# Seven-product MLP blocks: T1 and B22 weight quarters in large tiles instead of raw buffers

## The chip, the cores and the metric

The kernel runs on one core of a Trainium2 chip. The metric is device time in microseconds. Before the change three runs gave 951.79, 952.26 and 953.13 us; their median is 952.26 us. One more execution, recorded by the hardware profiler, took 955.36 us.

## The reference

One layer of a decoder trunk, batch 1, 512 tokens, width 1024, in float32. With h = RMSNorm(x):

- z = h @ W_in, cut into queries, keys, values and gates of a retention mixer (4 heads) and of a dilated windowed attention (3 groups of 4 heads);
- x = x + W_o(sigmoid(g_A) * (A @ W_A) + sigmoid(g_B) * (B @ W_B)), where A and B are the two mixers' results;
- x = x + W_down(relu(RMSNorm(x) @ W_up)^2), with W_up 1024 x 4096 and W_down 4096 x 1024;
- x = x + sigmoid(RMSNorm(x) @ W_pg) * (p @ W_pp), with p 512 x 256.

The change lies in the third line, the MLP.

## The kernel before, in words

**Precision.** Every float32 matrix product is made of three float32r products. A factor v is split into hi (v rounded to float32r, by ScalarE) and lo (v - hi, by VectorE); `mm3` (L259) issues hi·hi, hi·lo and lo·hi into the same accumulator (L262 to L264). In the profile `whi` and `wlo` are the parts of a weight unit (split at L250 and L251), `f` is a left factor's tile (split at L1300 and L1301), `pg` and `pa` are accumulators in PSUM, `x` is the residual stream, updated at L1286.

**Seven products.** Large products are done by a Strassen-like scheme (Winograd's form): both factors are cut into 2 x 2 quarters, and seven products of quarters or of their sums replace eight. On the weight's side the seven factors are B11, B21, B22, T1, T2, T3 and T4. They use storage in chains. T1 starts as the quarter B12, to which B11 is added; after T1's split B22 is accumulated into the same storage, which is T2; after T2's split B21 is accumulated, which is T4. B22 likewise becomes T3, when B12 is accumulated into it after its split. A factor of 512 x 512 is loaded and split in two units, u = 0 and u = 1, of 128 partitions x 1024 values (0.5 MB).

**Order.** In the MLP the products run in the order HALVES (L37): 1, 1, 5, 5, 2, 3, 3, 6, 6, 2, then 7 and 4 with both units at once. In units this is B11, B11, T1, T1, B21, B22, B22, T2, T2, B21, T3, T3, T4, T4, that is 14 units a block. The MLP has four rounds f, each with an up block (`up_products`, left factors h2, seven `f` tiles that all four rounds use) and a down block (`seven_gemm`, left factors U, seven `f` tiles made from the up block's results by relu and square). An up block turns the roles round: the weights are the stationary operand and the matmuls have 256 columns; in a down block the matmuls have 512 columns.

**Loading.** `plan_seven` (L171) writes the list of units. `fetch` (L199) allocates a unit's storage and issues its load on SyncE's queue (SP, L212). `ahead` (L217) keeps the splits two units ahead of use (three in some stretches, `AHEAD`), adds B11 into T1 on VectorE (L226, the `vector` argument holds "T1" in the MLP) and has GpSimd (POOL) issue the accumulating loads of a chain (L228). Such a load must wait for the split of what stood there before.

**Storage.** Raw units lie in the pool `wraw`: six buffers of 128 x 1024 values. Every one of the eight units of a block that are really loaded (B11, T1, B21, B22, two each) takes one; T1's stay taken until T4's split, B22's until T3's split. The splits' results lie in four buffers each (`wsp`). The pool `bigp` has 16 "big" tiles of 128 x 2048 values, from which the left factors h2 and U, the residual x (two tiles), zq, h3 and pp are taken.

**Who orders what.** The program is written against a planner. It places each instruction in the queue of its engine by priority in program order and by its own cost model, gives a tile a free slot of its pool, and adds the waits for a slot's former users. In some stretches (the update by w_o and the embedding's product, the last down block and all behind it) ScalarE and VectorE keep the written order (`manual_schedule`). SP holds only transfers and POOL in the MLP almost only the accumulating loads; both take theirs in order.

Of the kernel before, what the change touches and what calls it, by code (L numbers as in the profile page):

```python
# [11 lines left out]
F32 = mybir.dt.float32  # L12
# [5 lines left out]
P = 128  # L18
# [18 lines left out]
HALVES = ((1, 0), (1, 1), (5, 0), (5, 1)) + SEVEN[4:]  # L37
# [42 lines left out]
class Block:  # L80


    def __init__(self, ctx, tc, a):
        self.tc, self.nc, self.a = tc, tc.nc, a
        pool = lambda n, b, **k: ctx.enter_context(tc.tile_pool(name=n, bufs=b, **k))
        self.const = pool("const", 1)
        self.wraw = pool("wraw", 6)
        self.wsp = pool("wsp", 4)
        self.bigp = pool("bigp", 16)
        self.tmpp = pool("tmpp", 12)  # L90
        self.tabp = pool("tabp", 4)
        self.sm = pool("sm", 8)
        self.psg = pool("psg", 4, space=bass.MemoryType.PSUM)
        self.psa = pool("psa", 4, space=bass.MemoryType.PSUM)
        self.dram = pool("dram", 1, space=bass.MemoryType.DRAM)
        self.n = 0
        self.ev = 0
        self.clock = 0
        self.queue = []
        self.done = set()  # L100
        self.pinned = False
        self.hook = None
        self.chained, self.added = {}, {}
        self.spare = False
        self.plan, self.raws, self.loaded, self.used = [], [], [], 0

# [61 lines left out]
        for u in range(nk // 2):  # L168
            self.plan.append((w[r0 + 256 * u : r0 + 256 * (u + 1), c0 : c0 + 512], None if g0 is None else g0 + 2 * u))

    def plan_seven(self, w, r0, c1, c2, order, vector=()):  # L171

        cols = (c1, c2)
        q = lambda i, j, u: w[r0 + 512 * i + 256 * u : r0 + 512 * i + 256 * (u + 1), cols[j] : cols[j] + 512]
        n = len(self.plan)
        units = [(FACTOR[m], v) for m, u in order for v in ((0, 1) if u is None else (u,))]
        at = lambda name, u: n + units.index((name, u))
        for name, u in units:
            if name == "T1":
                src = q(0, 1, u) if name in vector else (q(0, 1, u), q(0, 0, u))  # L180
                if name in vector:
                    self.added[at("B11", u)] = at("T1", u), at("B11", u)
            elif name == "T4" and name in vector:
                self.added[max(at("B21", u), at("T2", u))] = at("T2", u), at("B21", u)
                src = (None, at("T2", u))
            elif name[0] == "B":
                src = q(int(name[1]) - 1, int(name[2]) - 1, u)
            else:
                prev, ij = {"T2": ("T1", (1, 1)), "T3": ("B22", (0, 1)), "T4": ("T2", (1, 0))}[name]
                k = at(prev, u)  # L190
                self.chained[k] = q(*ij, u)
                src = (None, k)
            self.plan.append((src, None))

    def plan_cols(self, w, c0, nk, g0=None):
# [3 lines left out]
    def fetch(self, n):  # L199
        while len(self.raws) < min(len(self.plan), n):  # L200
            src, g0 = self.plan[len(self.raws)]
            add = None
            if isinstance(src, tuple):
                src, add = src[0], src[1:]
            if src is None:
                self.raws.append((self.raws[add[0]][0], None))
                continue
            raw = self.wraw.tile([P, 1024], F32, tag="raw", name=self.nm("raw"))
            k = src.shape[0] // P
            raw = raw.rearrange("p (k n) -> p k n", k=k)  # L210
            rows = lambda v: v.rearrange("(k p) n -> p k n", p=P)
            self.nc.sync.dma_start(raw, rows(src))  # L212
            if add is not None:
                self.nc.gpsimd.dma_start(raw, rows(add[0]), accum_op=ALU.add)
            self.raws.append((raw, g0))
# [1241 lines left out]
    def make_plan(self):  # L1457
        a, w = self.a, self.w_in
        pairs = {1: (AV, AV + 512), 2: (RK, AV + 1024)}
        for g in range(NG):  # L1460
            for c in (AQ, AK):
                self.plan_rows(w, c + 512 * g, KD)
            if g:
                self.plan_seven(w, 0, *pairs[g], SEVEN, ("T1",))
        for c in range(2):
            self.plan_cols(w, RQ + 256 * c, KD)
        for c in (0, 512):
            self.plan_seven(w, 0, RV + c, RG + c, SEVEN, ("T1", "T4"))
        self.plan_mix()
        self.plan_seven(a["w_o"][0], 0, 512, 0, SEVEN)  # L1470
        for half in range(2):
            self.plan_rows(a["w_ple_proj"][0], 512 * half, 2)
        for f in range(NF // 2):
            self.plan_seven(a["w_up"][0], 0, 1024 * f + 512, 1024 * f, HALVES, ("T1",))
            self.plan_seven(a["w_down"][0], 1024 * f, 512, 0, HALVES, ("T1",))
        for half in range(2):
            self.plan_rows(a["w_ple_gate"][0], 512 * half, KD, g0=32)

# [38 lines left out]
```

## Time and profile before

| what | value |
|---|---|
| median of three runs | 952.26 us (951.79 to 953.13) |
| profiled execution, own time | 955.36 us |
| its span (first to last instruction) | 953.6 us |
| granted TensorE clock | 0.997 |
| TensorE busy | 943.3 us, 99% |
| VectorE busy | 718.4 us, 75% |
| ScalarE busy | 562.1 us, 59% |
| GpSimd busy | 159.5 us, 17% |
| DMA | 162.87 MB, mean 171 GB/s |

How to read it: times are microseconds; PE is TensorE's matmuls, PEld its weight loads, DVE VectorE, ACT ScalarE, POOL GpSimd and SP SyncE. A group of instructions is named by its line in the kernel, its engine and its tiles as out<-in. "A <- B" among the waits means that A's engine sat idle until B was done. The MLP's eight blocks lie between about 587 and 896 us of the span; the last product and the output follow.

### The profile page before, as it was taken

How to read it: one execution, taken by the hardware profiler on the slowest of the kernel's cores; microseconds unless marked ns; L12 is line 12 of the kernel's file. 1: busy time of each engine (PE TensorE's matmuls, PEld its weight loads, DVE VectorE, ACT ScalarE, POOL GpSimd, SP SyncE). 2: the span in 40 equal slices, each digit the busy share in tenths (PEclk: the TensorE clock that was granted, in tenths of full speed). 3: DMA queues.
4: the chain of work that ended last, by engine and by line, in shares of the span. 5: the costliest groups of instructions: out<-in, count | busy, mean ns of one | idle time of the engine just before them, and what ended most of it. 6: DMA issues, size and time to landing. Idle time of an engine off the chain costs nothing.

```text
span 953.6 us, 14325 instructions
## 1 busy us (share of the span) xinstructions
PE 943.3 (99%) x5357; PEld 826.2 (87%) x5357; DVE 718.4 (75%) x997; ACT 562.1 (59%) x1065; POOL 159.5 (17%) x140
## 2 busy tenths in 40 slices
PE   9999999999899999999999999999999999999998
PEld 6888888888788888999988888988998998998887
DVE  7789964766697849386937889799499689769953
ACT  5657775445745566576714446884494486467651
POOL 0322210222001112223012211111212302112100
PEclk9999999999999999999999999999999999999999
DMA  9953466258437645869737677868958968876911
GB/s 333 282 170 82 106 141 215 64 118 195 148 111 155 173 100 138 163 181 217 232 115 236 148 178 214 206 153 222 199 156 202 191 183 157 224 172 159 288 50 56
DMA packets 92549, 162.87 MB, mean 171 GB/s; under 512 B 8608, under 2 KB 20544, under 8 KB 92480
## 3 DMA queue, kind: packets, MB, share of 16 engines
q1 hardware_dynamic: 65168, 113.37, 36.4%
q0 software_dynamic: 23936, 46.14, 29.0%
q10 hardware_dynamic: 3376, 2.44, 0.9%
q8 instruction: 42, 0.69, 0.3%
q14 instruction: 27, 0.22, 0.1%
HBM read 153.49 MB, written 6.34 MB: 168 GB/s over the span
## 4 chain that ended last, share of the span: by engine, by line
PE 92%; DVE 3%; ACT 1%; issue 1%; DMA 1%; POOL 1%; SPq 0%; ACTq 0%; POOLq 0%; DVEq 0%
PE pg L264 25%; PE pg L262 25%; PE pg L263 25%; PE pa L264 3%; PE pa L263 3%; PE pa L262 3%; PE po L835 1%; PE ph L590 1%; DVE wlo L251 1%; PE pe L694 1%; PE sc L787 1%; PE ry L1083 1%; PE kv L1070 1%; PE ry L1085 1%; DVE ro L578 0%
## 5 line engine op out<-in xcount | busy, mean ns | idle before, releaser
L251 DVE TENSOR_TENSOR wlo<-raw,whi 128x1024 fp32r<-128x1024 f32 (+1 forms) x258 | 306.8, 1198 | 112.7 <-ACT whi L250 111.8
L250 ACT ACTIVATE whi<-raw 128x1024 fp32r<-128x1024 f32 (+1 forms) x257 | 266.3, 1041 | 212.1 <-PE pg L264 87.2
L263 PE MATMUL pg<-f,whi 128*128 128x256 f32 x384 | 108.7, 283 | 0.0
L264 PE MATMUL pg<-f,wlo 128*128 128x256 f32 x384 | 108.7, 283 | 0.0
L262 PE MATMUL pg<-f,whi 128*128 128x256 f32 x384 | 108.7, 283 | 0.0
L262 PE MATMUL pg<-whi,hh 128*128 128x512 f32 x248 | 98.6, 398 | 0.0
L264 PE MATMUL pg<-whi,hl 128*128 128x512 f32 x248 | 97.1, 392 | 0.0
L263 PE MATMUL pg<-wlo,hh 128*128 128x512 f32 x248 | 96.8, 390 | 0.0
L262 PE MATMUL pg<-whi,f 128*128 128x512 f32 x192 | 75.4, 393 | 0.0
L263 PE MATMUL pg<-wlo,f 128*128 128x512 f32 x192 | 74.8, 389 | 0.0
L264 PE MATMUL pg<-whi,f 128*128 128x512 f32 x192 | 74.8, 389 | 0.0
L262 PEld LDWEIGHTS pg<-f,whi 128*128 128x128 f32 x384 | 73.7, 192 | 0.2
L263 PEld LDWEIGHTS pg<-f,whi 128*128 128x128 f32 x384 | 73.7, 192 | 0.2
L264 PEld LDWEIGHTS pg<-f,wlo 128*128 128x128 f32 x384 | 73.7, 192 | 0.0
L228 POOL DMA_DIRECT2D raw<-in_w_in x32 | 38.9, 1216 | 197.8 <-DVE wlo L251 193.0
L264 PEld LDWEIGHTS pg<-whi,hl 128*128 128x128 f32 x248 | 46.6, 188 | 9.8
L263 PEld LDWEIGHTS pg<-wlo,hh 128*128 128x128 f32 x248 | 46.6, 188 | 9.2
L262 PEld LDWEIGHTS pg<-whi,hh 128*128 128x128 f32 x248 | 46.6, 188 | 9.2
L228 POOL DMA_DIRECT2D raw<-in_w_down x24 | 29.0, 1215 | 139.3 <-DVE wlo L251 108.2
L262 PE MATMUL pg<-whi,us 128*128 128x512 f32 x128 | 52.1, 407 | 0.0
L228 POOL DMA_DIRECT2D raw<-in_w_up x24 | 29.0, 1211 | 135.0 <-DVE wlo L251 124.7
L264 PE MATMUL pg<-whi,us 128*128 128x512 f32 x128 | 50.0, 391 | 0.0
(280 smaller groups left out, 2298.0 us busy)
## 6 DMA issues: line engine op xcount, KB each, us to landing
raw<-in_w_in SPq DMA_DIRECT2D x72, 512.0 KB, 4.1
raw<-in_w_in POOLq DMA_DIRECT2D x32, 512.0 KB, 6.2
raw<-in_w_up SPq DMA_DIRECT2D x32, 512.0 KB, 4.6
raw<-in_w_down SPq DMA_DIRECT2D x32, 512.0 KB, 4.6
raw<-in_w_up POOLq DMA_DIRECT2D x24, 512.0 KB, 6.6
raw<-in_w_down POOLq DMA_DIRECT2D x24, 512.0 KB, 5.9
x<-in_x SPq DMA_DIRECT2D x8, 512.0 KB, 8.2
raw<-in_w_ret_out SPq DMA_DIRECT2D x8, 512.0 KB, 3.8
```

Source lines behind the costliest of these rows:

```text
L228: self.nc.gpsimd.dma_start(raw, self.chained[i].rearrange("(k p) n -> p k n", p=P), accum_op=ALU.add)
L250: self.pin(nc.scalar.activation(R(hi[:, i]), raw[:, i], AF.Copy))
L251: nc.vector.tensor_tensor(R(lo[:, i]), raw[:, i], hi[:, i], op=ALU.subtract)
L262: t.matmul(ps, sh, mh, start=first, stop=False, skip_group_check=more)
L263: t.matmul(ps, sh, ml, start=False, stop=False, skip_group_check=more)
L264: t.matmul(ps, sl, mh, start=False, stop=last, skip_group_check=more)
L590: self.nc.tensor.transpose(ps[:, t * P : (t + 1) * P], rots[t][:, h * HD : (h + 1) * HD], self.ident)
L694: self.nc.tensor.transpose(ps[:, k * P : (k + 1) * P], e[:, k * P : (k + 1) * P], self.ident)
L787: nc.tensor.matmul(sc[:, h * P : (h + 1) * P], qT[:, h, rs], kT[:, h, rs], start=True, stop=True)
L835: nc.tensor.matmul(po[:, h * P : (h + 1) * P], v[:, vt, h * HD : (h + 1) * HD], pt, start=b == 0, stop=b == len(blocks) - 1)
L1070: nc.tensor.matmul(ps, kd[:, n, hs], v[:, n, c], start=True, stop=True)
L1083: nc.tensor.matmul(y, sT[0][:, r], v[:, i, c], start=True, stop=i == 0)
```

## The change

`plan_seven` gets one more argument, `wide`, a list of factor names. A unit of such a factor is noted in `self.wide` with the plan position of the factor's first unit. `fetch` then doesn't allocate a `wraw` buffer for it: the factor's first unit allocates one big tile (128 x 4 x 512 values), and each of its two units takes one half of it, rearranged to 128 x 1024 values. The MLP's plans pass ("T1", "B22"). T2, T3 and T4 stand in the storage of T1 and B22, as before, so they go along. The pools keep their sizes (six raw buffers, 16 big tiles); loads, additions and accumulating loads are the same ones in the same program order.

```diff
@@ plan_seven
-    def plan_seven(self, w, r0, c1, c2, order, vector=()):
+    def plan_seven(self, w, r0, c1, c2, order, vector=(), wide=()):
...
                 self.chained[k] = q(*ij, u)
                 src = (None, k)
+            if name in wide:
+                self.wide[len(self.plan)] = at(name, 0), u
             self.plan.append((src, None))
@@ fetch
-            raw = self.wraw.tile([P, 1024], F32, tag="raw", name=self.nm("raw"))
+            if len(self.raws) in self.wide:
+                n, u = self.wide[len(self.raws)]
+                if n not in self.pairs:
+                    self.pairs[n] = self.big("raw")
+                raw = self.pairs[n][:, 2 * u : 2 * u + 2].rearrange("p a b -> p (a b)")
+            else:
+                raw = self.wraw.tile([P, 1024], F32, tag="raw", name=self.nm("raw"))
@@ make_plan
-            self.plan_seven(a["w_up"][0], 0, 1024 * f + 512, 1024 * f, HALVES, ("T1",))
-            self.plan_seven(a["w_down"][0], 1024 * f, 512, 0, HALVES, ("T1",))
+            self.plan_seven(a["w_up"][0], 0, 1024 * f + 512, 1024 * f, HALVES, ("T1",), ("T1", "B22"))
+            self.plan_seven(a["w_down"][0], 1024 * f, 512, 0, HALVES, ("T1",), ("T1", "B22"))
```

More of the change, by code (lines that the diff above doesn't have):

```diff
@@ L103, in __init__ @@
         self.chained, self.added = {}, {}
+        self.wide, self.pairs = {}, {}
         self.spare = False
```

## The prediction

> **What bounds the kernel now.** I read the engine totals and the chain of waits on the page first. "pg" and "pa" are the accumulators of the matrix products.
>
> ```profile
> PE 943.3 (99%) x5357; PEld 826.2 (87%) x5357; DVE 718.4 (75%) x997; ACT 562.1 (59%) x1065; POOL 159.5 (17%) x140
> ...
> PE 92%; DVE 3%; ACT 1%; issue 1%; DMA 1%; POOL 1%; SPq 0%; ACTq 0%; POOLq 0%; DVEq 0%
> ```
>
> TensorE is busy for 943.3 of 953.6 us and makes 92% of the chain that ends last. The change only touches the MLP, so next I read the busy time in single blocks: the first up block, the first down block, and the next up and down (their borders are where the matmuls change from 256 to 512 columns).
>
> ```profile
> 586.87:627.18 40.31, 40.31 (x337) 40.31 (x336) 33.53 (x44) 35.25 (x58) 7.26 (x6) 1.00 0.83 205
> 627.18:665.29 38.11, 38.11 (x171) 31.54 (x169) 37.17 (x48) 21.61 (x28) 7.28 (x6) 1.00 0.85 194
> 665.29:705.60 40.31, 40.31 (x337) 40.31 (x336) 26.39 (x28) 26.43 (x37) 7.25 (x6) 1.00 0.77 183
> 705.60:743.97 38.37, 38.37 (x171) 31.38 (x169) 37.10 (x47) 21.80 (x29) 7.25 (x6) 1.00 0.82 191
> ```
>
> The columns are: length, busy PE, PEld, DVE, ACT and POOL, the granted clock (1.00), the share and GB/s of the DMA engines. PE is busy to the last hundredth. A busy PE could hide slow matmuls, so I also read the starts of matmuls in a down block and in an up block:
>
> ```profile
> 799.95 0.39 PE L262 MATMUL pg<-whi,f 128*128 128x512 f32 x1
> ...
> 804.94 0.39 PE L263 MATMUL pg<-wlo,f 128*128 128x512 f32 x1
> ```
>
> ```profile
> 589.74 0.28 PE L262 MATMUL pg<-f,whi 128*128 128x256 f32 x1
> ...
> 592.98 0.28 PE L262 MATMUL pg<-f,whi 128*128 128x256 f32 x1
> ```
>
> From 799.95 to 804.94 there are 22 starts after the first, 0.227 us apart; from 589.74 to 592.98 there are 27, 0.120 us apart. A down block has 14 weight units of 12 matmuls: 168 x 0.227 = 38.1 us. An up block has 14 of 24: 336 x 0.120 = 40.3 us. Both are the measured lengths, so these blocks hold nearly no hidden idle time. The exception is the second down block, 38.37 against 38.11: 0.26 us lost. What TensorE waits for from 560 us on is little (two answers of the waits view, for PE and for its weight loads):
>
> ```profile
> PE pg L262 <- ACT pp L533: 0.2, 1, 0.2
> ```
>
> ```profile
> PEld pg L262 <- ACT pp L533: 0.6, 1, 0.6
> PEld pg L263 <- DVE wlo L256: 0.5, 1, 0.5
> PEld pg L262 <- issue: 0.3, 1, 0.3
> PEld pg L262 <- ACT whi L250: 0.3, 1, 0.3
> PEld pg L262 <- DVE x L1286: 0.3, 1, 0.3
> ```
>
> None of these names a weight load. Against them stands what SyncE's queue waits for between 582 and 862 us:
>
> ```profile
> SPq L212 <- DVE wlo L251: 238.0, 53, 13.9
> ```
>
> The weight loads do wait for a free raw buffer: 53 times, 238 us. But no engine on the chain pays for it. The buffers are scarce, and scarce off the path.
>
> **The change, part by part.** *What is moved.* In each of the eight MLP blocks, T1 (B12 loaded, B11 added by DVE at L226, B22 and then B21 accumulated into it by POOL) and B22 (with B12 accumulated later) leave the raw pool. Each becomes one half-pair of a "big" tile. B11 and B21 stay in the six raw buffers. The instructions stay:
>
> ```profile
> raw<-in_w_up SPq DMA_DIRECT2D x32, 512.0 KB, 4.6
> raw<-in_w_down SPq DMA_DIRECT2D x32, 512.0 KB, 4.6
> raw<-in_w_up POOLq DMA_DIRECT2D x24, 512.0 KB, 6.6
> raw<-in_w_down POOLq DMA_DIRECT2D x24, 512.0 KB, 5.9
> ```
>
> There are 64 loads on SP, 48 accumulations on POOL and 16 additions of about 1.22 us on DVE before and after, of the same shapes. Removed and added work: 0 us. Compute operands remain contiguous rows of 1024 values, so I take no change in durations.
>
> *What is freed.* A block asks for four raw buffers instead of eight. B11 and B21 can therefore be loaded up to a block and a half ahead, and the 238 us of SP waits shrink or become waits for big tiles. Worth on the path: only PE idle time counts. Upper bound of a gain: 0.26 us (second down block) + 0.2 + 0.6 + 0.5 + 0.3 x 3 = 2.5 us if all of it vanished and none were counted twice. But the pp rows and the last stage's wlo L256 do not involve these buffers, and the 0.3 of x L1286 is probably part of the 0.26. What the change could reach is 0.26 + 0.3 (issue) + 0.3 (whi), about 0.9 us. I take 0.2.
>
> *What is added: demand on the big tiles.* There are 16. During the MLP seven hold the left factors of up, two the residual x; the seven left factors of down take the rest, exactly 16. T1 and B22 make 18, so something must wait. Big tiles seem to be handed out in program order: pp is written back by 596 us at the latest (589.6, its last store, and at most 8.0 to landing), but is loaded again into big tiles only at 895 us, just behind the first writes of h3, which stands before it in the program.
>
> ```profile
> L534 SPq DMA_DIRECT2D pp_dram<-pp x8: 319/320/350, 579.5 to 589.6; - x8
> L1439 SPq DMA_DIRECT2D pp<-pp_dram x2: 421/439/457, 895.0 to 895.5; - x2
> ...
> DMA to landing us min/median/max: 2.0/3.4/8.0
> ```
>
> So the splits of the last left factors wait for TensorE to finish products 1 and 5, and the next T1 for the end of product 3's first use (seven units into the block). That is 5.4, 10.9 and 19.1 us after the block's start (2, 4 and 7 units of 12 x 0.227 = 2.72 us). Today the last of those splits run at 715.59, 10 us in, and are used by products 7 and 4, 27 and 33 us in; the wait moves them by about a microsecond. Behind them on ScalarE stand the splits of the coming weight units:
>
> ```profile
> 715.59 1.66 ACT L1300 ACTIVATE f<-r 128x512 fp32r<-128x512 f32 x3
> ...
> 730.31 1.07 ACT L250 ACTIVATE whi<-raw 128x1024 fp32r<-128x1024 f32 x1 [1.65 <-PE pg L264]
> ```
>
> The unit split at 730.31 is T4's first half, product 4's first operand:
>
> ```profile
> 735.17 1.06 ACT L250 ACTIVATE whi<-raw 128x1024 fp32r<-128x1024 f32 x1 [3.79 <-DVE wlo L251]
> ...
> 736.26 1.23 DVE L251 TENSOR_TENSOR wlo<-raw,whi 128x1024 fp32r<-128x1024 f32 x1 [1.20 <-ACT whi L250]
> ...
> 737.41 0.74 DVE L1286 SCALAR_TENSOR_TENSOR x<-pg,f,x 128x512 f32<-128x512 f32 x1
> ...
> 738.30 0.47 PE L262 MATMUL pg<-whi,f 128*128 128x512 f32 x1
> ```
>
> TensorE first needs it at 738.30: 8.0 us after 730.31, less 1.07 and 1.23 of splitting, leaves 5.7 us of cover. Cost taken: 0; without that cover, the wait itself.
>
> *The tightest place.* The same rows show it. T4's second half is split at 735.17, 3.79 us after ScalarE fell idle. The row names wlo, but the accumulation that fills this unit landed just then. It is the second of the pair that POOL issues at 723.40; the next answer is that line's landings from 720 to 740:
>
> ```profile
> 723.40 2.49 POOL L228 DMA_DIRECT2D raw<-in_w_down  x2 [0.90 <-DVE wlo L251]
> ```
>
> ```profile
> DMA to landing us min/median/max: 5.6/6.3/10.4
> ```
>
> The second starts 1.2 us or so behind the first, near 724.7; with the longest landing, 10.4, that is 735.1. DVE takes its instructions in order, so the update x stands behind that wlo, and product 4 adds into the bank that x must have read. PE starts at 738.30 with 0.47 instead of 0.39. So the landing of T4's accumulation reaches TensorE with no slack in this block. DVE is busy 37.17 of 38.11 us in the first down block, so 0.94 us is a fair estimate of the slack elsewhere. What is late here is paid.
>
> Why 10.4 instead of 5.6? SP issues seven loads from 715.96 to 740.81, in a burst once B22's raw buffers come free:
>
> ```profile
> 715.96 24.85 SPq L212 DMA_DIRECT2D raw<-in_w_up  x7
> ```
>
> After the change the raw loads of this burst go earlier, and T1's pair goes when product 3's big tile is free: 705.6 + 19.1 = 724.7, the very moment of T4's accumulations; B22's pair follows with product 6's tile at 9 units, 730.1. One load fewer to one load more beside the accumulation: 0.52 MB at 194 GB/s is 2.7 us either way. Bounds: minus 0.26 us in all to plus 2.7 x 3 = 8.1 us for three blocks (in the fourth no further MLP weights are loaded). I take +0.2, near the lower end, because the same bytes pass per block and the burst loses B11's loads while it gains T1's.
>
> The Trainium skill, "DMA: Bandwidth & Descriptors", section "Queues, rings and completion order", says that each DMA engine takes turns between the queues it has work for, packet by packet. By it an accumulation next to loads gets about half of the engines, so, as an estimate, 5.6 us becomes about 10; the row of 10.4 agrees, and by that rule T1's pair at 724.7 speaks against the change.
>
> *The ends.* The first T1 pair, loaded now from 564.08, could wait for a big tile. Even issued when w_o's matmuls end and its left factors' tiles come free (574.62, the first matmul of the next product), the pair would land by 574.6 + 2 x 4.6 = 583.8, against the first addition at 581.57; that addition's unit is the third of the block, used at 586.87 + 2 x 2.88 = 592.6. Cost 0.
>
> ```profile
> 564.08 9.58 SPq L212 DMA_DIRECT2D raw<-in_w_up  x4
> ```
>
> ```profile
> 574.62 0.39 PE L262 MATMUL pg<-whi,ph 128*128 128x512 f32 x1
> ```
>
> ```profile
> 581.57 1.22 DVE L226 TENSOR_TENSOR raw<-raw,raw 128x1024 f32<-128x1024 f32 x1
> ```
>
> *Sum.* The profiled execution took 955.36 us, 1.76 more than its span and 3.1 more than the median of 952.26. 955.36 + 0 (instructions) - 0.2 (stalls) + 0.2 (accumulations) = 955.4; as a median, 952.3 us.
>
> **The rivals.** *Late accumulations (slower).* At product 4 of the first three down blocks one more load lies beside T4's accumulation: 2.7 us later, less 0.94 of slack, 1.76 x 3 = 5.3 us: 957.6. It decides from the point where T4's second landing is more than 0.94 us later in its block than now. For: DVE at 37 of 38 us, 10.4 against 5.6. Against: equal bytes.
>
> *Big tiles run out (slower).* If a T1 takes the tile that the last left factor needs, that split waits until 19.1 instead of about 11 us; 8.2 less 5.7 of cover is 2.5 a block: 959.8. Against: program order puts T1 behind it.
>
> *The stalls go (slightly faster).* 952.26 - 0.9 = 951.4, still no difference that can be told.
>
> *It does not do what it says.* If T1's place in the order holds SP's later loads back, nothing is earlier: 952.3.
>
> *Hidden headroom (faster).* If the array idled wherever no weights are loaded, a down block would hold 38.11 - 31.54 = 6.6 us, four of them 26: 926. The even starts, 0.227 us apart, speak against it. The Trainium skill, "Perfetto Trace Analysis", section "Identifying the Most-Contended Engine", holds weight-load time for the better measure than matmul time; by that rule there is room, by the starts there is none.
>
> **How the numbers follow.** A difference under 0.2% (1.9 us) can't be told from none here. Chances: forecast 0.58 and "does not do it" 0.06 (952.3), stalls go 0.10 (951.4), late accumulations 0.19 (957.6), tiles run out 0.04 (959.8), headroom 0.03 (926). Faster: 0.03 and 0.04 of the tails of the first three: 0.07. Slower: 0.23 less 0.03 of milder cases, 0.20. Same: 0.73. The range goes from 951.0, below the case of 951.4, to 957.0, which takes in most of the late accumulations; its bound of 8.1 us (960.4) and the headroom stay outside.
>
> **What would show it.** Right: blocks of 40.3 and 38.1 us; no PE wait that names a raw or a left factor; SP's 238 us much smaller. Wrong on accumulations: down blocks over 39 us with x L1286 ahead of the first matmul of product 4, and T4's landing over 11 us. Wrong on tiles: ScalarE's f L1300 waiting for PE. What I could not see is the order that the planner gives ScalarE and VectorE once tiles are released at other times; a bad order there makes the prediction wrong.

## The result, and the profile after

The changed kernel takes 958.71 us (median of four runs, 957.54 to 959.62) against 952.23 us for the kernel before: a ratio of 1.0066 with a 95% interval from 1.0049 to 1.0084. It is 6.5 us slower. The forecast was 952.3 us with a range up to 957.0, so the result lies outside.

The profiled execution of the changed kernel took 957.94 us, 0.8 below its median; that of before was 3.1 above its own. The two spans (956.2 and 953.6 us) are therefore not compared. The blocks are. Lines of the changed kernel are those of before plus 9 (`whi` L259, `wlo` L260, `mm3` L271 to L273, the load L221, the addition L235, the accumulation L237, `x` L1295).

Engine totals and the chain of waits on the page of the changed kernel:

```profile
PE 944.2 (99%) x5357; PEld 824.9 (86%) x5357; DVE 719.2 (75%) x997; ACT 561.4 (59%) x1065; POOL 159.6 (17%) x140
...
PE 86%; DMA 5%; DVE 4%; issue 3%; ACT 2%; POOL 1%; SPq 0%; POOLq 0%; ACTq 0%; DVEq 0%
```

No engine does more work: the counts are the same and every busy time is within 1.3 us. But PE makes 86% of the chain instead of 92%, and transfers 5% instead of 1%. Next, the same blocks as in the prediction (length, then busy PE, PEld, DVE, ACT and POOL, clock, DMA share, GB/s), with the sum over the first seven blocks; first the changed kernel, then the sum of before:

```profile
583.52:626.00 42.48, 41.13 (x337) 40.51 (x336) 31.86 (x41) 34.35 (x57) 7.29 (x6) 1.00 0.74 182
626.00:666.15 40.15, 38.70 (x170) 31.39 (x169) 38.75 (x49) 22.61 (x29) 7.28 (x6) 1.00 0.88 220
666.15:706.46 40.31, 40.31 (x337) 40.31 (x336) 26.41 (x29) 26.38 (x36) 7.25 (x6) 1.00 0.70 158
706.46:745.22 38.76, 38.35 (x170) 31.46 (x169) 37.38 (x47) 21.78 (x28) 7.28 (x6) 1.00 0.88 216
...
sum 281.02, PE 277.52 PEld 255.75 DVE 224.71 ACT 178.58 POOL 50.84; mean PE 39.65 PEld 36.54 DVE 32.10 ACT 25.51 POOL 7.26
```

```profile
sum 275.83, PE 275.83 PEld 255.69 DVE 224.13 ACT 178.80 POOL 50.78; mean PE 39.40 PEld 36.53 DVE 32.02 ACT 25.54 POOL 7.25
```

Seven blocks take 281.02 - 275.83 = 5.19 us longer. Of this the first up block has 42.48 - 40.31 = 2.17, the first down block 40.15 - 38.11 = 2.04, the second down block 38.76 - 38.37 = 0.39 and the third 38.68 - 38.11 = 0.57; the other up blocks have nothing. From the start of the fourth down block to the last matmul another 0.75 us are lost (86.92 against 86.17). Together 5.94 of the 6.48 us; the rest is within the scatter of single executions. So the loss lies in the MLP, and nearly all of it in four blocks. The waits of TensorE from 560 to 960 us (engine, line, what it waited for: us in total, times, longest):

```profile
PE pg L271 <- DVE x L1295: 1.4, 3, 0.7
PE pg L273 <- DVE wlo L260: 1.3, 2, 0.8
PE pa L272 <- DVE wlo L260: 0.7, 1, 0.7
```

Before, PE had one wait here, 0.2 us for pp. Now the splits of weight units (wlo) and x are late. Three of the waits are x ahead of product 4, the "tightest place" of the prediction. This is that place in the second down block (706.46 to 745.22; ahead of 736.57 ScalarE had been idle):

```profile
736.57 1.06 ACT L259 ACTIVATE whi<-raw 128x1024 fp32r<-128x1024 f32 x1 [3.23 <-PE pg L273]
...
737.67 1.22 DVE L260 TENSOR_TENSOR wlo<-raw,whi 128x1024 fp32r<-128x1024 f32 x1 [1.29 <-ACT whi L259]
...
738.81 0.74 DVE L1295 SCALAR_TENSOR_TENSOR x<-pg,f,x 128x512 f32<-128x512 f32 x1
...
739.70 0.47 PE L271 MATMUL pg<-whi,f 128*128 128x512 f32 x1 [0.41 <-DVE x L1295]
```

T4's second half is split at 736.57, VectorE makes wlo at 737.67, then x at 738.81, and PE starts product 4 at 739.70, 0.80 us after the start of the matmul before (738.90). What released ScalarE is the landing of T4's second accumulation: the row names a product of PE, but this landing, worked out below, comes 0.1 us ahead of the split. The two accumulations are issued from 724.5 to 725.8 us; the landings of that line, and SP's transfers at that time:

```profile
L237 POOL DMA_DIRECT2D raw<-in_w_down x2: 1213/1218/1222, 724.5 to 725.8; - x2
...
DMA to landing us min/median/max: 7.6/9.1/10.7
```

```profile
725.72 0.92 SPq L221 DMA_DIRECT2D raw<-in_w_up  x2
728.39 0.37 SPq L221 DMA_DIRECT2D raw<-in_w_down  x1
731.16 0.89 SPq L221 DMA_DIRECT2D raw<-in_w_up  x2
```

725.8 + 10.7 = 736.5. T1's pair went at 725.72 and B22's at 731.16, that is 19.3 and 24.7 us into the block. The other large loss is in the first up block. Its B22 pair (L221, issued 590.0 to 590.8) against the same pair before (L212, 573.3 and 582.8), and what ScalarE and TensorE do with it:

```profile
L221 SPq DMA_DIRECT2D raw<-in_w_up x2: 729/802/875, 590.0 to 590.8; - x2
...
DMA to landing us min/median/max: 6.9/7.2/7.5
```

```profile
L212 SPq DMA_DIRECT2D raw<-in_w_up x2: 367/375/383, 573.3 to 582.8; - x2
...
DMA to landing us min/median/max: 4.5/4.6/4.6
```

```profile
597.03 1.06 ACT L259 ACTIVATE whi<-raw 128x1024 fp32r<-128x1024 f32 x1 [0.66 <-DMA raw<-in_w_up]
```

```profile
598.14 0.39 PE L271 MATMUL pg<-f,whi 128*128 128x256 f32 x1
...
599.40 0.39 PE L273 MATMUL pg<-f,wlo 128*128 128x256 f32 x1 [0.51 <-DVE wlo L260]
```

Product 3's first unit is due at 597.9; its weights land at 596.9, and their parts are ready 0.2 and 0.7 us late. This is 1.1 us. Another 1.1 follow at unit 12 of the same block, and 1.0 at unit 4 of the first down block. The accumulations that fill B22's and T1's storage again are pushed back with it: POOL issues four in one run at 599.7.

```profile
599.71 5.01 POOL L237 DMA_DIRECT2D raw<-in_w_up  x4 [12.05 <-DVE wlo L260]
```

Last, SyncE's queue, between 582 and 862 us, as in the prediction:

```profile
SPq L221 <- DVE wlo L260: 201.5, 21, 17.5
SPq L221 <- PE pg L273: 31.0, 10, 8.0
SPq L221 <- DVE raw L235: 15.5, 7, 2.5
```

Its waits have not gone: 201.5 + 31.0 + 15.5 = 248 us against 238. Fewer, longer and for other things.

### The profile page after: what moved, and what is told of

It is laid out like the page before. It is cut to its first block, busy times and chain, and to the rows that moved or that the text cites. A ratio compares the mean times of both kernels' runs of the same rounds, so it can differ in the third digit from the quotient of the medians.

```text
span 956.2 us, 14288 instructions
## 1 busy us (share of the span) xinstructions
PE 944.2 (99%) x5357; PEld 824.9 (86%) x5357; DVE 719.2 (75%) x997; ACT 561.4 (59%) x1065; POOL 159.6 (17%) x140
## 4 chain that ended last, share of the span: by engine, by line
PE 86%; DMA 5%; DVE 4%; issue 3%; ACT 2%; POOL 1%; SPq 0%; POOLq 0%; ACTq 0%; DVEq 0%
PE pg L271 23%; PE pg L273 23%; PE pg L272 23%; PE pa L273 3%; PE pa L271 3%; PE pa L272 3%; DMA raw<-in_w_up 2%; DMA raw<-in_w_down 2%; PE po L844 1%; PE ph L599 1%; DVE wlo L260 1%; ACT whi L259 1%; PE sc L796 1%; PE ry L1092 1%; PE pe L703 1%
## 5 line engine op out<-in xcount | busy, mean ns | idle before, releaser
L260 DVE TENSOR_TENSOR wlo<-raw,whi 128x1024 fp32r<-128x1024 f32 (+1 forms) x258 | 306.7, 1200 | 115.0 <-ACT whi L259 113.8
L259 ACT ACTIVATE whi<-raw 128x1024 fp32r<-128x1024 f32 (+1 forms) x257 | 266.1, 1041 | 214.6 <-PE pg L273 85.6
L273 PE MATMUL pg<-f,wlo 128*128 128x256 f32 x384 | 108.7, 283 | 1.3 <-DVE wlo L260 1.3
L271 PE MATMUL pg<-f,whi 128*128 128x256 f32 x384 | 108.8, 283 | 0.1
L271 PE MATMUL pg<-whi,hh 128*128 128x512 f32 x248 | 98.6, 398 | 0.0
L273 PE MATMUL pg<-whi,hl 128*128 128x512 f32 x248 | 96.8, 390 | 0.0
L271 PE MATMUL pg<-whi,f 128*128 128x512 f32 x192 | 75.3, 393 | 1.4 <-DVE x L1295 1.4
L273 PEld LDWEIGHTS pg<-f,wlo 128*128 128x128 f32 x384 | 73.6, 192 | 1.7 <-DVE wlo L260 1.7
L273 PE MATMUL pg<-whi,f 128*128 128x512 f32 x192 | 74.8, 390 | 0.0
L271 PEld LDWEIGHTS pg<-f,whi 128*128 128x128 f32 x384 | 73.7, 192 | 0.4 <-ACT whi L259 0.3
L237 POOL DMA_DIRECT2D raw<-in_w_in x32 | 38.9, 1217 | 194.5 <-DVE wlo L260 189.8
L273 PEld LDWEIGHTS pg<-whi,hl 128*128 128x128 f32 x248 | 46.6, 188 | 9.9
L271 PEld LDWEIGHTS pg<-whi,hh 128*128 128x128 f32 x248 | 46.6, 188 | 9.2
L237 POOL DMA_DIRECT2D raw<-in_w_down x24 | 29.1, 1220 | 142.7 <-DVE wlo L260 113.6
L271 PE MATMUL pg<-whi,us 128*128 128x512 f32 x128 | 52.2, 408 | 0.0
L237 POOL DMA_DIRECT2D raw<-in_w_up x24 | 29.0, 1219 | 137.2 <-DVE wlo L260 137.0
L273 PE MATMUL pg<-whi,us 128*128 128x512 f32 x128 | 50.0, 391 | 0.0
```

The source lines that it names most:

```text
L237: self.nc.gpsimd.dma_start(raw, self.chained[i].rearrange("(k p) n -> p k n", p=P), accum_op=ALU.add)
L259: self.pin(nc.scalar.activation(R(hi[:, i]), raw[:, i], AF.Copy))
L260: nc.vector.tensor_tensor(R(lo[:, i]), raw[:, i], hi[:, i], op=ALU.subtract)
L271: t.matmul(ps, sh, mh, start=first, stop=False, skip_group_check=more)
L273: t.matmul(ps, sl, mh, start=False, stop=last, skip_group_check=more)
```

## The experiments

In each kernel the blocks are judged as above: a down block without loss is 38.11 us long, an up block 40.31. Of each edit the lines that act are shown; lines that only set up their variables are left out. The kernel before was measured again beside each set of experiments, and the ratios are to those runs.

**One factor at a time.** Only T1 in big tiles (shown), or only B22, with `("B22",)` in the same place.

```diff
-            self.plan_seven(a["w_up"][0], 0, 1024 * f + 512, 1024 * f, HALVES, ("T1",), ("T1", "B22"))
-            self.plan_seven(a["w_down"][0], 1024 * f, 512, 0, HALVES, ("T1",), ("T1", "B22"))
+            self.plan_seven(a["w_up"][0], 0, 1024 * f + 512, 1024 * f, HALVES, ("T1",), ("T1",))
+            self.plan_seven(a["w_down"][0], 1024 * f, 512, 0, HALVES, ("T1",), ("T1",))
```

> Only T1 goes to big tiles, B22 stays in the raw buffers. A: six raw quarters for each block leave the raw loads hardly any lead over the pairs, so the first blocks lose under 0.5 us together. B: T1's pair still is loaded beside T4's accumulations: 0.5 to 0.9 us ahead of product 4 in each of three down blocks, as in the changed kernel. Both together: 954 us. If neither, 958 to 959 us.

> Only B22 goes to big tiles, T1 stays in the raw buffers. B: T1's loads wait for raw buffers as before, so nothing new lies beside T4's accumulations; ahead of product 4 at most 0.3 us a block is lost. A: the B22 pair of the first up block can stand behind raw loads of later blocks as in the changed kernel; up to 2 us lost there. Both together: 952.5 to 954.5 us. If the big tiles' number is what costs (16 asked for by fewer pairs), the losses are halved in every place: 955.5 us.

With T1 alone: 955.42 us, ratio 1.0029 (1.0019 to 1.0040). With B22 alone: 976.21 us, 1.0252 (1.0228 to 1.0277). The first up block and the first two down blocks of the kernel with T1 alone:

```profile
583.47:623.78 40.31, 40.31 (x337) 40.30 (x336) 32.93 (x42) 35.00 (x57) 7.26 (x6) 1.00 0.80 197
623.78:662.86 39.08, 38.38 (x171) 31.48 (x169) 37.68 (x48) 21.86 (x28) 7.29 (x6) 1.00 0.79 191
703.17:742.21 39.04, 38.39 (x170) 31.47 (x169) 37.42 (x47) 21.78 (x28) 7.28 (x6) 1.00 0.78 188
```

T1 alone loses 0.9 to 1.0 us in each of the first three down blocks, all of it ahead of product 4, and nothing in the first up block. The loss of the first up block belongs to B22. B22 alone loses the most, and by a different way: VectorE takes its queue in order and stands at the addition of B11 to T1, whose load landed late because it had to wait for a raw buffer. That addition in VectorE's timeline, in the second up block of that kernel, and the block itself:

```profile
698.88 1.23 DVE L235 TENSOR_TENSOR raw<-raw,raw 128x1024 f32<-128x1024 f32 x1 [5.68 <-DMA raw<-in_w_down]
```

```profile
670.65:715.16 44.51, 42.13 (x338) 41.89 (x336) 26.60 (x29) 26.11 (x36) 7.29 (x6) 0.96 0.65 144
```

The updates r (L1334) behind that addition start at 701.16, and PE waits for them. So the two halves of the change aren't independent: with T1 in big tiles as well, this stall doesn't appear.

**SP in program order.** The six raw buffers let later blocks' B11 and B21 run ahead of B22 in SP's queue; this kernel takes all loads of the MLP in program order, each placed behind the last without a wait for it.

```diff
+            ins = self.nc.sync.dma_start(raw, rows(src))
+            if len(self.raws) >= min(self.wide):
+                if self.last is not None:
+                    self.tc.add_manual_dep(ins.ins, self.last.ins.name, mybir.DependencyInfo(
+                        mybir.DependencyClass.NoSync, mybir.DependencyReason.DATA), reason="load order")
+                self.last = ins
```

> The changed kernel, with the weight loads of the MLP issued in the order of the program (each load is placed behind the one before it; nothing waits for a landing). Theory A, head of SP's queue: the planner had written the raw quarters of later blocks ahead of the T1 and B22 pairs, and these quarters wait for raw buffers, so the pairs come late. Then the first up block's B22 pair goes at least 7 us earlier than at 590 us, the losses there (2.2 us) and at the first down block's B21 (1.0 us) go, and the time is about 955.5 us. Theory B, contention alone: T1's pair still comes beside T4's accumulations, the losses ahead of product 4 (0.95, 0.65, 0.54 us) stay and so does the time, 958 to 959 us. Theory C, order of ScalarE and VectorE: no forecast for a single place; the losses move to others and the sum stays near 6 us.

Measured: 960.49 us, 1.0082 (1.0061 to 1.0102), no better than the change. The first up block takes 43.44 us. SP's queue in that kernel:

```profile
580.23 6.28 SPq L549 DMA_DIRECT2D pp_dram<-pp  x4
586.60 3.73 SPq L222 DMA_DIRECT2D raw<-in_w_up  x3
```

B22's pair goes 2 us earlier than in the change, straight behind the stores of pp. Its first load stands at the head of SP's queue from 586.60 and waits until 587.9 for TensorE to free the big tile; its second starts at 588.8. The pair now takes some 9 us to land instead of 7, beside more loads, and so lands hardly earlier (596.7 against 596.9): 0.9 us are still lost at product 3, and 2.1 more at unit 10. A raw load at the head of SP's queue (589.52 in the change) thus held the pair back by about 2 us at most, and these 2 us don't bring the time back; the rest of the delay against 573.3 is the wait for the tile. Ahead of product 4 this kernel loses 2.0, 1.0 and 0.9 us in the first three down blocks, no less than the change.

**Round 0 left alone.** Big tiles only from the second round on.

```diff
-            self.plan_seven(a["w_up"][0], 0, 1024 * f + 512, 1024 * f, HALVES, ("T1",), ("T1", "B22"))
-            self.plan_seven(a["w_down"][0], 1024 * f, 512, 0, HALVES, ("T1",), ("T1", "B22"))
+            self.plan_seven(a["w_up"][0], 0, 1024 * f + 512, 1024 * f, HALVES, ("T1",), ("T1", "B22") if f else ())
+            self.plan_seven(a["w_down"][0], 1024 * f, 512, 0, HALVES, ("T1",), ("T1", "B22") if f else ())
```

> Only the rounds 1 to 3 of the MLP are wide; round 0 is as before. A: the 2.2 us of the first up block and the 1.0 us of the first down block go, unless the first wide block (up, round 1) shows the same late B22 pair, then 1 to 2 us come back there; 954 to 957 us. B: one of three tight places ahead of product 4 goes (0.95 us); 957.7 us.

Measured: 960.50 us, 1.0083 (1.0063 to 1.0103). The first down block, which itself uses no big tiles here, is the worst of all:

```profile
624.97:669.12 44.15, 39.78 (x170) 32.52 (x169) 37.48 (x48) 21.50 (x28) 7.29 (x6) 0.96 0.85 218
```

The first up block, also without big tiles, loses 1.3 us ahead of unit 12, where PE waits for an update r. T4's two accumulations of the first down block took 12.2 and 15.1 us to land. Five loads of later blocks had been issued within 2 us, 10.3 to 12.3 us into the block, 6 us before the accumulations.

**An extra load in the kernel before.** The kernel before, unchanged but for one copy of 0.5 MB of weights to a DRAM tile that nobody reads, placed in each down block beside T4's accumulations (it waits for the wlo of T2's first half). Nothing is left out.

```diff
+                if i in self.beside:
+                    ins = self.nc.sync.dma_start(self.unread, self.chained[i])
+                    self.tc.add_manual_dep(ins.ins, self.low.ins.name, mybir.DependencyInfo(
+                        mybir.DependencyClass.Sync, mybir.DependencyReason.DATA), reason="beside T4")
```

> The kernel before (no large tiles), with one copy of 0.5 MB more in each down block, from DRAM to DRAM and read by nobody, issued on SP when T4's accumulations are due (about 18 us into the block). Contention theory: T4's second accumulation lands 2 to 3 us later than the 28.4 to 29.5 us of the kernel before, and what it lands after about 29.3 us is lost ahead of product 4, one for one: 1 to 3 us in each of three down blocks, 956 to 960 us. Rival (the loss comes from the order that the planner gives ScalarE and VectorE, not from transfers): that order stays nearly the same here, nothing is lost, 952 to 953.5 us.

Measured: 960.6 us, 1.0089 (1.0072 to 1.0106). SP issues the copy at 721.93 us in the second down block, and the block grows from 38.37 to 39.79:

```profile
704.18:743.97 39.79, 38.53 (x171) 31.38 (x169) 37.24 (x48) 21.87 (x29) 7.25 (x6) 1.00 0.85 201
```

```profile
L230 POOL DMA_DIRECT2D raw<-in_w_down x2: 1213/1218/1222, 722.3 to 723.5; - x2
...
DMA to landing us min/median/max: 8.8/10.1/11.5
```

One transfer beside the accumulations, and no big tile anywhere, makes the same kind of loss at the same place: 1.4, 1.5 and 1.9 us ahead of product 4 in the three blocks. The two traces have the MLP's instructions on ScalarE and VectorE in the same order, one by one, so a changed order is not the cause. These 4.8 us are not the whole 8.3: the first and the last up block lose another 0.6 and 0.7 us, where PE waits for an update r behind T1's addition, which waited 1.2 and 1.9 us for its load. The first of these two comes ahead of any copy, and its cause is not shown.

**B22 of the first up block left raw.**

```diff
-            self.plan_seven(a["w_up"][0], 0, 1024 * f + 512, 1024 * f, HALVES, ("T1",), ("T1", "B22"))
+            self.plan_seven(a["w_up"][0], 0, 1024 * f + 512, 1024 * f, HALVES, ("T1",), ("T1", "B22") if f else ("T1",))
```

> The changed kernel, but the B22 of the first up block stays in raw buffers. Theory: of the 6 us, 2.2 us are that pair's late load (issued at 590 us instead of 573 and 583), because its large tile is handed out only after the tiles of the up left factors. Then the first up block has its 40.3 us again, and the 1.0 us at the first down block's fifth unit goes too if it is that delay's echo: 955.5 us. If the late pair is not the cause: 958.5 us.

Measured: 956.27 us, 1.0040 (1.0025 to 1.0055), 2.5 us less than the change. The first up block and the first two down blocks:

```profile
583.46:623.77 40.31, 40.31 (x338) 40.31 (x336) 32.51 (x42) 35.11 (x57) 7.25 (x6) 1.00 0.80 195
623.77:664.23 40.46, 38.70 (x171) 31.36 (x169) 38.03 (x48) 21.60 (x28) 7.28 (x6) 1.00 0.86 214
704.54:743.46 38.92, 38.39 (x170) 31.46 (x169) 37.43 (x47) 21.78 (x28) 7.28 (x6) 1.00 0.88 216
```

All 2.2 us of the first up block are back. In the first down block the loss at unit 4 shrinks from 1.0 to 0.3 us, but 2.0 instead of 0.95 are now lost ahead of product 4, where the accumulation lands at 31.3; in the other two down blocks it is 0.8 and 1.0 instead of 0.65 and 0.56. So of the 2.5 us only 1.3 show in the seven blocks of the two profiled executions.

**T1's first half behind T4.** In each later block the load of T1's first half waits until the previous block's last T4 accumulation has landed; once on the change as it is, once with the first B22 left raw too. `self.filled` is the latest accumulating load.

```diff
+            i = len(self.raws)
+            if i in self.wide and self.wide[i] == (i, 0) and i - 2 > min(self.wide) and i - 2 in self.added:
+                self.tc.add_manual_dep(ins.ins, self.filled.ins.name, mybir.DependencyInfo(
+                    mybir.DependencyClass.Sync, mybir.DependencyReason.DATA), reason="behind T4")
```

> The changed kernel, with the load of T1's first half waiting until the T4 accumulation of the block before has landed; the loads behind it in SP's queue wait too. Contention theory: T4's second accumulation lands before 29.3 us into the down blocks, and the losses ahead of product 4 (0.95, 0.65, 0.56 us) go; the first up block's 2.2 us and the 1.0 us in the first down block stay: 956.5 us. Rival: the losses ahead of product 4 stay, 958.5 us; if the later loads are now too late, 960 us or more, with waits on raw in other places.

> Both edits together: the first B22 in raw buffers and T1's first half behind T4. If the two causes are separate and are the whole of it, 953 to 953.5 us, within 0.2% of the kernel before. If one cause shifts into the other, 955 to 957 us.

Measured: 958.77 us, 1.0071 (1.0054 to 1.0088), and 955.32 us, 1.0032 (1.0021 to 1.0043). In the first of them T4's second accumulation still lands 30.0 us into the second down block, and 0.7 us are lost. SP's queue shows why: the wait moved one half of T1 and, behind it, B22's pair; T1's other half still goes 19.3 us into the block, and a load of a later block 2.7 us behind it.

```profile
726.16 0.37 SPq L221 DMA_DIRECT2D raw<-in_w_up  x1
728.83 0.37 SPq L221 DMA_DIRECT2D raw<-in_w_down  x1
736.96 1.39 SPq L221 DMA_DIRECT2D raw<-in_w_up  x3
```

Three of the five loads issued near the accumulation are gone, and it is no earlier. T1's other half, which is left, is issued within 0.1 us of it (19.35 us into the block).

**Both halves of T1 behind T4, and all of the block's first loads.** With the first B22 left raw: in the one kernel (shown) both halves of T1 wait for the previous block's T4; in the other (`at % 14 < 9`) B11, T1, the first half of B21 and B22 do. `self.filled` is here T4's second accumulation alone.

```diff
+            at = len(self.raws) - min(self.wide) + 2
+            if self.filled is not None and 14 <= at < 112 and at % 14 in (2, 3):
+                self.tc.add_manual_dep(ins.ins, self.filled.ins.name, mybir.DependencyInfo(
+                    mybir.DependencyClass.Sync, mybir.DependencyReason.DATA), reason="behind T4")
```

> The same as the last, but only the two halves of T1 of each later block wait for the previous block's second T4 accumulation; B11, B21 and B22 are issued as the planner likes. In an earlier run only T1's first half waited, and loads issued at +19.3 and +21.9 us of the second down block stayed beside T4's accumulation, which landed at +30.1. Theory: the load at +19.3 is T1's second half and goes; the one at +21.9 (B11 of a later block) stays; landing at about +28.5 to +29.3 us and at most 0.1 us lost at product 4 of the second and third down blocks, about 954 us. Rival (late by themselves): landing at +29.9 and 0.6 us lost, about 956 us.

> Kernel with T1 and B22 in big tiles, except for the first up block's B22 (which by itself took 956.27 us), and with one thing added: the loads of B11, T1 and B22 and of the first half of B21 of each later block wait for the landing of the previous block's second T4 accumulation, so that no weight load runs beside the T4 accumulations. Nothing is left out. Theory (the accumulations share the DMA engines with loads issued earlier): T4's second accumulation lands at +26 to +28 us of each down block, 7 to 9 us after its issue at +19.4 instead of 10.7, so no loss ahead of product 4 in the first three down blocks (now .3 to 2.0); about 953.0 us if the next blocks' first units, loaded from +28 on, still come in time (B11 is wanted at +38). Rival (the accumulations are late by themselves, issued behind one another on POOL's queue): landing at +29.9 or later and 0.5 to 1.0 us lost in each of the first three down blocks as before, about 956 us.

With both halves of T1 held: 953.77 us, ratio 1.0005 (0.9992 to 1.0019): no difference from before. Its trace and that of the kernel with only the first B22 raw (1.0040) have the same order on ScalarE and VectorE, so what lies between these two is the loads alone. The first up block and the first three down blocks, and T4's landings in the second down block:

```profile
582.88:623.19 40.31, 40.31 (x337) 40.31 (x336) 32.65 (x42) 35.08 (x57) 7.25 (x6) 1.00 0.81 196
623.19:661.52 38.33, 38.33 (x170) 31.46 (x169) 37.13 (x47) 21.87 (x28) 7.28 (x6) 1.00 0.89 216
701.83:739.94 38.11, 38.11 (x170) 31.55 (x169) 37.60 (x48) 21.78 (x28) 7.28 (x6) 1.00 0.90 221
780.25:819.06 38.81, 38.58 (x170) 31.39 (x169) 36.52 (x46) 21.78 (x28) 7.26 (x6) 1.00 0.84 207
```

```profile
DMA to landing us min/median/max: 6.2/7.5/8.8
```

T4's second accumulation takes 8.8 us instead of 10.7, and the second down block has no loss at all, less than before the change. The third still loses 0.7: 0.15 ahead of product 4, and 0.5 a unit later, where PE waits for an update x. That x stands in VectorE's queue behind T1's addition, which waits 1.4 us for the load that was held:

```profile
814.26 1.23 DVE L240 TENSOR_TENSOR raw<-raw,raw 128x1024 f32<-128x1024 f32 x1 [1.42 <-DMA raw<-in_w_up]
```

With everything held, no load runs beside the accumulations, and in the second down block they land in 6.3 and 7.6 us; ahead of product 4 nothing is lost in any of the first three. The rival, that the accumulations are late by themselves, falls. Yet that kernel takes 966.92 us, 1.016 (1.0114 to 1.0207): eight loads start in one burst, T1's addition waits for them, and VectorE stands in its queue as in the kernel with B22 alone. Its row in the first up block:

```profile
620.90 1.23 DVE L240 TENSOR_TENSOR raw<-raw,raw 128x1024 f32<-128x1024 f32 x1 [5.21 <-DMA raw<-in_w_down]
```

**What all kernels say together.** For each kernel, from its trace: the loads issued in a down block from 10 us on, those ahead of T4's second accumulation plus those behind it until its landing; the landing in us from the block's start, less what PE had already lost in the block; and what PE loses ahead of product 4. It is the second down block throughout, and the first for the kernel with round 0 left alone.

| kernel | loads | landing | loss |
|---|---|---|---|
| all of the first loads held | 0 + 0 | 27.26 | 0 |
| T1 held | 1 + 1 | 28.17 | 0 |
| before | 1 + 3 | 29.44 | 0.12 |
| first B22 raw, T1's first half held | 2 + 1 | 29.89 | 0.56 |
| the change | 2 + 4 | 29.98 | 0.65 |
| T1's first half held | 2 + 1 | 30.03 | 0.70 |
| first B22 raw | 2 + 4 | 30.11 | 0.79 |
| B22 alone | 3 + 2 | 30.12 | 0.80 |
| T1 alone | 3 + 3 | 30.22 | 0.90 |
| in program order | 1 + 9 | 30.35 | 1.03 |
| before, one copy more | 2 + 4 | 30.83 | 1.51 |
| round 0 left alone | 5 + 4 | 33.95 | 5.27 |

The loss is the landing less 29.3, to 0.05 us, in all but the last row (4.65; there slower matmuls after the pause are in the 5.27). So what is paid ahead of product 4 is the lateness of this one landing.

The landing goes with what starts close to the accumulation. With no load it is 27.3. Where the next load follows 2.6 us behind, it is 28.2 and 29.4. Where T1's first load goes 0.1 us ahead, it is 29.9 to 30.1 with one or with four loads behind it, and 30.35 with nine. (Most of these rows have one more load, some 9 us ahead.) Three loads about 8 us ahead give as much (B22 alone and T1 alone), five of them 34.0.

Whether the close load is ahead or behind doesn't decide. In the third down block of the change T1's first load goes 0.06 us behind T4's second accumulation, which takes 10.7 us there as in the second block; in the kernel in program order nothing is issued ahead of it from 10 us on and ten loads behind, and it takes 10.8, against 8.0 with everything held. T4's first accumulation, too, takes 7.6 us in the second down block of the change, where T1's first load follows 1.2 us behind it, and 6.2 us with T1 held. So the number of loads ahead is no price list.

Two things are not settled. The copy from DRAM to DRAM costs more than T1's loads; it reads and writes there, but it also starts 1.6 us ahead of the accumulation, and no run separates the two. And 1 + 3 lands later than 1 + 1, but the same issue times gave landings from 28.2 to 29.5 us in the three blocks of the kernel with T1 held, so that the row alone doesn't show a price of the later loads.

## Why the prediction was wrong, point by point

**What bounds the kernel** was read rightly: PE has no slack, the blocks are 40.3 and 38.1 us where nothing waits, and no added or removed work over 1.3 us shows in any engine's total.

**What is freed.** The prediction held that the 238 us of SP's waits would shrink. They are 248 us. The raw buffers that come free are taken by loads of later blocks, and the queue stands again, for PE to release big tiles too. No wait of TensorE shows a cost of that by itself, but with it the loads start at other times, in pairs.

**Demand on the big tiles.** T1's pair was put at 19.1 us of the down block and B22's at 24.5: measured 19.3 and 24.7. The splits of the last left factors cost nothing that the waits show; the 5.7 us of cover were enough, and the rival of big tiles running out did not come. Its sign came in small: ScalarE's f waited for PE twice, 1.3 us in all, and PE not for it. (The last store of pp, 589.6 plus at most 8.0, gives 597.6 and not 596; it landed at 595.8, and nothing hangs on it.)

**The tightest place** was the right place, with the right mechanism, and was given the wrong size. The term was +0.2 us for the accumulations, chosen near the lower end "because the same bytes pass per block". Measured are 0.95, 0.65 and 0.56 us in the first three down blocks against 0, 0.12 and 0 before: 2.0 us. Equal bytes were no argument. What counts is which loads start close to T4's last accumulation, and the change brings T1's pair there; with T1 held back all of it is gone but 0.15 us. The "burst" of seven loads that the prediction read was none either: the row from 715.96 merges loads that started one by one over 25 us, the second at 727.25 and the others 1.7 to 3.7 us apart, so that only three of the seven started within the accumulation's 10.4 us. The slack was also uneven: taken as 0.94 us from VectorE's busy time, it was 29.3 - 28.36 = 0.94 in the first down block, 0.55 in the third, and none in the second. The rival of late accumulations had the sign and the place, and 957.6 us is near the result, but for half of its reason: it priced a landing 2.7 us later, while it moved by 1.9, 0.5 and 1.1, so its 5.3 us were 2.0. That its 957.6 lies near the measured time is partly luck, for the other 4 us come from places that it doesn't name. The signs that the prediction set for it were too high as well: the first down block alone is over 39 us, and no landing in the first three takes more than 10.75.

The rule drawn from the Trainium skill, "DMA: Bandwidth & Descriptors", section "Queues, rings and completion order", that engines take turns between queues, gave about 10 us for an accumulation beside loads as an estimate and spoke against the change. The runs agree: 7.6 us with no load beside it, 10.7 in the change. By turns a load issued just behind the accumulation should slow it as well as one just ahead, and the third down block agrees with that too: 10.7 us with T1's first load 0.06 us behind. The runs show the sharing; by which rule the DMA engines share they don't show.

**The ends** is the step that failed by omission. It looked at the first T1 pair, found 9 us of room and took 0. The first B22 pair was not looked at. Its tile comes free later, the pair goes at 590.0 instead of 573.3, and lands 1 us before it is due. That costs 2.17 us in the first up block. Through the accumulations and splits behind it, it also costs 0.7 at unit 4 of the first down block, though what is won there goes to product 4 while T1 stays where it is. Left raw, 2.5 us of the median are back. If big tiles are handed out in program order, as the prediction held, this could have been looked for: the pair follows the left factors of the same block in the program, and in the kernel in program order its first load did wait for TensorE, until 587.9.

**What could not be seen** was named: the order on ScalarE and VectorE. It has a share. At unit 12 of the first up block the accumulation lands at 617.3, but ScalarE splits it only at 619.48, behind the updates of r, and at unit 4 of the first down block wlo stands behind f, r and x. VectorE's order differs from the kernel before in many places, but it does so in the kernel with T1 held as well, and that one's seven blocks are only 0.7 us longer than before: outside the first up block the new order costs little. In the first up block the order and the late pair change together, and there its own price is not shown. The loss from the fourth down block on (0.75 us, most of it at T1's first unit, where PE waits 0.5 us for wlo) comes with T1 in big tiles: the kernels with T1 alone and with T1 held have it too, the kernel with B22 alone has not. That wlo stands behind others on VectorE; why it does wasn't tested.

**The sum** of what the trace shows: 2.2 (first B22, first up block) + 1.0 (unit 4 of the first down block) + 2.0 (ahead of product 4) + 0.75 (from the fourth down block on) = 5.95, which is the 5.94 measured from block to block, against +0.2 - 0.2 in the prediction.

## What to carry to other kernels

More room for loads is not free: loads that may start earlier will, and then share the DMA engines with whatever transfer is on the critical path; so find the transfer that lands with the least slack, and ask of each change which loads it puts beside that one. With the first B22 left raw, holding back two loads per block behind that transfer undid the loss; holding back seven cost more than it saved, because an engine that works in order then stood at the first instruction that needed them. And when a buffer moves to another pool, look at the first use of every factor that moves, not only of the first one.

## What the runs showed of the hardware that was not expected

TensorE's clock fell after a pause of 2.7 us, and not after each such pause. In the kernel with B22 alone PE stood from 699.3 to 702.0 us; the windows of that time show the granted clock (the number ahead of the last two) at 0.53 for some 3 us afterwards, with matmuls 0.21 us apart instead of 0.12. After a slightly longer pause at 782.8 (2.87 us from start to start of two matmuls, against 2.66) it stayed at 1.00:

```profile
699.40:702.00 2.60, 0.22 (x3) 0.05 (x1) 2.60 (x4) 0.13 (x1) 0.00 (x0) 1.00 0.00 0
702.90:706.20 3.30, 3.30 (x18) 3.30 (x18) 3.08 (x5) 3.30 (x8) 0.00 (x0) 0.53 0.42 142
...
782.80:785.60 2.80, 0.23 (x2) 0.04 (x2) 2.80 (x4) 0.09 (x1) 0.00 (x0) 1.00 0.00 0
785.70:789.00 3.30, 3.30 (x28) 3.30 (x29) 3.30 (x6) 3.30 (x7) 0.00 (x0) 1.00 0.14 29
```

So a wait of 2.7 us costs, some of the time, one or two more (as an estimate 1.4 here: 15 matmuls, each 0.09 us later than at the full clock). The Trainium skill, "TensorE: Matmul & The Clock Gate", section "What's actually happening", gives half the clock after an idle window of about 3.4 us; here 2.7 us were enough in some cases, and in the MLP of the change itself, whose pauses are all under 1.2 us, the clock stayed at 1.00.
